# Gates stored sixteen keys to a row, and sixteen gathered rows moved to a later stage, in a decoder block on one core

## The chip, the cores and the metric

The kernel runs on one core of a Trainium2 chip. The metric is the device time of one execution in microseconds (us); lower is better. The engines are PE (TensorE, matmul; its weight loads are shown as PEld), DVE (VectorE), ACT (ScalarE), POOL (GpSimd) and SP (SyncE, which here only issues DMAs). Each engine works through its own instructions in order; 16 DMA engines move the data.

## The reference

One decoder block on x of shape (1, 512, 1024): an RWKV-7 group beside sliding-window attention, then PEER, a mixer that retrieves experts by product keys. The change lies in PEER alone, on 4 blocks of 128 tokens:

```python
def block(x_b):
    q = (x_b @ wq).reshape(-1, H, 2, PEER_HALF).astype(f32)
    s = jnp.einsum('thcd,hcnd->thcn', q, subkeys.astype(f32))
    s_top, i_top = lax.top_k(s, K)
    cand_s = (s_top[:, :, 0, :, None] + s_top[:, :, 1, None, :]).reshape(-1, H, K * K)
    cand_i = (i_top[:, :, 0, :, None] * PEER_N_KEYS + i_top[:, :, 1, None, :]).reshape(-1, H, K * K)
    best_s, best_pos = lax.top_k(cand_s, K)
    idx = jnp.take_along_axis(cand_i, best_pos, axis=-1).reshape(-1, H * K)
    gate = jax.nn.softmax(best_s, axis=-1).reshape(-1, H * K).astype(x_b.dtype)
    u = u_tab[idx]
    act = jax.nn.gelu(jnp.einsum('td,ted->te', x_b, u), approximate=False)
    return jnp.einsum('te,ted->td', gate * act, v_tab[idx])
```

H is 8 heads, K 16 choices, so 128 experts of 16384 for each token. An expert's number is 128 times its first key plus its second key.

## The kernel before

PEER is computed in two ways at once. **Tokens 128 to 511** (three blocks, `ND` = 384 tokens) are computed densely: every one of the 16384 experts is multiplied with every token, and a gate, zero where the expert was not chosen, takes out the rest. The experts are handled in 128 blocks of 128. For block b the *u-product* (`up_product`, tile pA, lines L176 to L178 in the helper `mm3_`) multiplies the 128 vectors u with the 384 tokens: 24 matmuls, since every factor is split into a high and a low part (`split`, L166 on ACT for the high part uh, L167 on DVE for the low part ul). A Gelu (L969) makes act of it. In the main part, act times gate is `w_` (`weigh`, L1312 on POOL), which is split into wh and wl, and is multiplied with the vectors v of the block, split into vh and vl (`accumulate`, L1357 to L1359, tile acc, 18 matmuls a block).

**Tokens 0 to 127** are computed by gathering: for each of the 128 choices j, `gather(j)` lets POOL issue an indirect DMA that fetches one row of 1024 numbers for each token (L1169, 512 KB in all, four buffers), first from u (j from 0 to 127), then from v (128 to 255). `gathered(j)` multiplies it on DVE: a u row with h2g (L1182, tile scr, sum into ac), a v row with ac, added to x (L1180).

The order on each engine is the order in which the code is written (a manual schedule). The stages from 580 us on are:

- **The gates' stage** (`for n in range(8 * NTC)`, 96 units). Unit n makes the gates of four tokens: DVE writes one-hot tiles O (L1228) and P (L1233), three units ahead; PE multiplies them in eight matmuls (L1255, tile pG); ACT copies the result into the tile gst (L1256). After eight units a chunk of 32 tokens, 2 MB, is written to DRAM by SP (L1266). Between the units run 69 steps of u-products made ahead (a step is 12 matmuls, so two make one block; SP loads its u at L796), whose act is kept in SBUF or spilled to DRAM (actd, acts). And `EARLY` gathered rows are asked for, spread evenly over the 96 units; each is multiplied three requests later.
- **The turn**: the last chunk is written in eight pieces (one at L1266, seven at L1336), ten more steps of u-products run, and the first gates (`gate_load`, L1296, tile gts, 12 loads for four blocks) and v (L1304) are loaded.
- **The main part** (`for b in range(127)`): each iteration loads three blocks ahead (`load`), splits block b + 1 (`prepare_block`), weighs block b + 2, accumulates block b, and computes the u-product of block 22 + b where it was not made ahead: 64 of the iterations, the others are single ones. Then come the rows asked for one iteration earlier, and new requests up to `upto(b)`, which shares 256 - `EARLY` rows out over blocks 0 to 120, twice as many to an iteration with a u-product as to a single one. After the last rows the norm of tokens 0 to 127 follows, and at the end that of the others (`residual`).

The gates in DRAM are an array (n, 128, GW x TC) for each chunk: second key in the middle, and GW first keys with TC = 32 tokens each side by side in a row; `NG` = 128 / GW. GI = 4 first keys are read at once, 512 bytes a partition.

Of the kernel before, what the change touches and what calls it, by code (L numbers as in the profile page):

```python
# [64 lines left out]
SPILL = [RING + (i * (128 - RING)) // NSPILL for i in range(NSPILL)]  # L65
AHEAD_UP = list(range(RING)) + SPILL

EARLY = 44


def peer_block_kernel(tc, A, out, dbg=None, stop=None):
    with ExitStack() as ctx:
        _emit(ctx, tc, A, out, dbg or {}, stop)


def _emit(ctx, tc, A, out, dbg, stop):
# [1026 lines left out]
    def steps(gen, n):  # L1103
        for _ in range(n):
            next(gen, None)
# [60 lines left out]
    def gather(j):  # L1166
        r_ = gp_.tile([128, D], F32, name="row", tag="row", bufs=4)
        w_, jj = j // 128, j % 128
        GP.indirect_dma_start(r_, None, A["vB"].rearrange("b p d -> (b p) d") if w_ else A["u"],  # L1169
                              bass.IndirectOffsetOnAxis(ap=ix[:, w_, jj:jj + 1], axis=0))  # L1170
        rows[j] = r_

    def gathered(j):
# [7 lines left out]
        else:  # L1181
            V.scalar_tensor_tensor(scr, r_, 1.0, h2g, op0=OP.mult, op1=OP.mult, accum_out=ac[:, jj:jj + 1])  # L1182


    TC, GI, GW = 32, 4, 8
    NG = 128 // GW
    NTC = ND // TC

    NG0 = 2
    gd = [[nc.dram_tensor(f"gates{t}_{g0}", (n, 128, GW * TC), F32, kind="Internal").ap() for g0, n in  # L1190
           (((0, NG0), (NG0, NG - NG0)) if t == NTC - 1 else ((0, NG),))] for t in range(NTC)]
    hot = {}
# [46 lines left out]
    for n in range(3):  # L1239
        one_hots(n)  # L1240
    def pieces(ci):
        return ([(0, NG0)] + [(g, 2) for g in range(NG0, NG, 2)]) if ci == NTC - 1 else [(0, NG)]

    done = asked = 0
    left = 2 * len(AHEAD_UP) - sum(UPS1) - sum(UPST) - BEHIND
    for n in range(8 * NTC):
        one_hots(n + 3)
        O, P = hot.pop(n)
        ci, t4 = n // 8, n % 8
        if t4 == 0:  # L1250
            gst = tk.tile([128, NG, GW, TC], F32, name="gst", tag="gst", bufs=2)
        p = psT.tile([128, 4, 128], F32, name="pG", tag=("sel", "pq", "psc")[n % 3], bufs=2)
        for u in range(4):
            for i in range(2):
                mm(p[:, u, :], O[:, u // 2, 0, :, u % 2], P[:, u // 2, i, :, u % 2], start=i == 0, stop=i == 1)  # L1255
        SC.activation(gst[:, :, :, t4 * 4:t4 * 4 + 4].rearrange("p n g t -> p (n g) t"),  # L1256
                      p.rearrange("p t e -> p e t"), AF.Copy, scale=1.0 / GS)
        if t4 == 7:

            writes = []  # L1260
            for g0, n_ in pieces(ci):
                d = gd[ci][g0 >= NG0 and ci == NTC - 1]
                d0 = NG0 if d.shape[0] == NG - NG0 else 0
                writes.append((d[g0 - d0:g0 - d0 + n_].rearrange("n p x -> p n x"),
                               gst[:, g0:g0 + n_].rearrange("p n g t -> p n (g t)")))
            SY.dma_start(*writes.pop(0))  # L1266
        steps(ups, (n + 1) * left // (8 * NTC) - n * left // (8 * NTC))
        while asked < (n + 1) * EARLY // (8 * NTC):
            gather(asked)
            asked += 1  # L1270
            if asked > 3:
                gathered(done)
                done += 1
# [11 lines left out]
    def upto(b):  # L1285

        return min(256, EARLY + (256 - EARLY) * sum(cost[:b + 1]) // sum(cost[:LASTG + 1]))

    vs, ws, gts = {}, {}, {}

    def gate_load(g):
        gts[g] = pv_.tile([128, NTC, GI, TC], F32, name="gts", tag="gts", bufs=2)
        for i in range(NTC):
            n, part = g // (GW // GI), g % (GW // GI)
            d, n = (gd[i][0], n) if len(gd[i]) == 1 or n < NG0 else (gd[i][1], n - NG0)
            SY.dma_start(gts[g][:, i], d[n, :, part * GI * TC:(part + 1) * GI * TC].rearrange("p (g t) -> p g t", t=TC))  # L1296
# [191 lines left out]
```

## Time and profile before

| what | value |
|---|---|
| time, median of 3 runs | 1629.78 us (1628.6 to 1633.54) |
| the profiled execution | 1630.73 us |
| its span, first to last instruction | 1629.0 us |
| granted TensorE clock, mean of the span | 0.995 |
| PE busy | 1572.6 us, 97% |
| DVE busy | 1286.1 us, 79% |
| POOL busy | 742.4 us, 46% |
| ACT busy | 652.5 us, 40% |
| moved by DMA | 371.18 MB, 228 GB/s over the span |

The busy times are sums over the whole span; what bounds a stage is read from the stage. Windows give them for a stretch, a timeline the single instructions, and the waits say for what an engine stood still.

### The profile page before, as it was taken

To read this page: it belongs to the slowest core of one execution; us is meant where nothing else is said; L and a number is where in the kernel's file an instruction comes from. 1 tells how busy PE (TensorE), PEld (TensorE's weight loads), DVE (VectorE), ACT (ScalarE), POOL (GpSimd) and SP (SyncE) were. 2 spreads that over 40 slices of the span, in tenths; PEclk is the share of its full clock that TensorE was granted. 3 is DMA by queue.
4 is the path that set the end of the run, shared out by engine and by line. 5 is a ranking of instruction groups with operands and counts; after the bars stand their busy time and mean duration, and the time that the engine had idled before them with its cause. 6 is when DMAs were issued, how large, how long until landed. Compare 5 with 4: busy or idle time off the path is not lost.

```text
span 1629.0 us, 30768 instructions
## 1 busy us (share of the span) xinstructions
PE 1572.6 (97%) x11869; PEld 1366.7 (84%) x11869; DVE 1286.1 (79%) x2497; ACT 652.5 (40%) x1092; POOL 742.4 (46%) x711
## 2 busy tenths in 40 slices
PE   7999999899999889999999999999999999999997
PEld 4777777797999888888988888888888888888886
DVE  6666567756899999999677788777878877887896
ACT  5333345544444344454433333333333333333334
POOL 5121123244676512222155555555655556556582
PEclk9999999999999999999999999999999999999999
DMA  4111110333232269999999888889998988989793
GB/s 143 53 42 42 59 48 2 129 124 103 79 104 91 98 214 336 348 323 354 320 345 351 304 309 320 322 299 316 331 308 301 333 312 303 321 303 339 236 311 136
DMA packets 180548, 371.18 MB, mean 228 GB/s; under 512 B 17840, under 2 KB 102320, under 8 KB 180144
## 3 DMA queue, kind: packets, MB, share of 16 engines
q1 hardware_dynamic: 137488, 226.71, 40.6%
q0 software_dynamic: 36864, 134.23, 22.9%
q10 hardware_dynamic: 6048, 8.26, 1.4%
q8 instruction: 93, 1.52, 0.4%
q14 instruction: 55, 0.45, 0.1%
HBM read 333.62 MB, written 35.52 MB: 227 GB/s over the span
## 4 chain that ended last, share of the span: by engine, by line
PE 50%; DVE 11%; DMA 3%; issue 1%; ACT 1%; POOL 1%; SPq 0%; DVEq 0%; ACTq 0%
PE acc L1359 10%; PE acc L1358 10%; PE acc L1357 10%; PE pA L178 7%; PE pA L176 7%; PE pA L177 7%; DVE O L1228 3%; DVE ul L167 2%; DVE scr L1182 2%; DVE P L1233 2%; DMA u<-in_uT_dram 2%; DMA row<-in_vB_dram,ix 1%; DMA v<-in_vB_dram 0%; PE pG L1255 0%; POOL row L1169 0%
## 5 line engine op out<-in xcount | busy, mean ns | idle before, releaser
L178 PE MATMUL pA<-h2hi,ul 128*128 128x384 f32 x1024 | 346.2, 338 | 9.9 <-DVE ul L167 5.6
L176 PE MATMUL pA<-h2hi,uh 128*128 128x384 f32 x1024 | 350.3, 342 | 1.5 <-ACT actd L969 1.5
L177 PE MATMUL pA<-h2lo,uh 128*128 128x384 f32 x1024 | 344.1, 336 | 0.0
L1169 POOL DMA_INDIRECT row<-in_u_dram,ix x128 | 175.2, 1369 | 285.7 <-DVE scr L1182 247.7
L1359 PE MATMUL acc<-vl,wh 128*128 128x512 f32 x768 | 300.3, 391 | 1.5 <-DVE vl L167 1.5
L1358 PE MATMUL acc<-vh,wl 128*128 128x512 f32 x768 | 300.0, 391 | 0.2 <-DVE wl L167 0.2
L1357 PE MATMUL acc<-vh,wh 128*128 128x512 f32 x768 | 298.9, 389 | 1.3 <-ACT vh L166 1.3
L1169 POOL DMA_INDIRECT row<-in_vB_dram,ix x128 | 196.1, 1532 | 141.1 <-DVE x L1180 115.7
L167 DVE TENSOR_TENSOR vl<-v,vh 128x1024 fp32r<-128x1024 f32 x128 | 213.9, 1672 | 35.2 <-ACT vh L166 34.4
L178 PEld LDWEIGHTS pA<-h2hi,ul 128*128 128x128 f32 x1024 | 192.8, 188 | 14.8 <-DVE ul L167 10.5
L176 PEld LDWEIGHTS pA<-h2hi,uh 128*128 128x128 f32 x1024 | 193.0, 188 | 4.7 <-ACT actd L969 1.6
L177 PEld LDWEIGHTS pA<-h2lo,uh 128*128 128x128 f32 x1024 | 193.2, 189 | 3.0
L1180 DVE SCALAR_TENSOR_TENSOR x<-row,ac,x 128x1024 f32<-128x1024 f32 x128 | 173.2, 1353 | 7.9 <-DMA row<-in_vB_dram,ix 6.0
L1359 PEld LDWEIGHTS acc<-vl,wh 128*128 128x128 f32 x768 | 144.1, 188 | 32.2 <-DVE vl L167 2.2
L1357 PEld LDWEIGHTS acc<-vh,wh 128*128 128x128 f32 x768 | 144.2, 188 | 30.0 <-ACT vh L166 1.6
L1358 PEld LDWEIGHTS acc<-vh,wl 128*128 128x128 f32 x768 | 144.1, 188 | 29.4 <-DVE wl L167 0.6
L1182 DVE SCALAR_TENSOR_TENSOR scr<-row,h2g 128x1024 f32<-128x1024 f32 x128 | 158.2, 1236 | 1.3
L166 ACT CAST uh<-u 128x1024 fp32r<-128x1024 f32 x128 | 133.9, 1046 | 62.2 <-PE pA L177 29.5
L167 DVE TENSOR_TENSOR ul<-u,uh 128x1024 fp32r<-128x1024 f32 x109 | 134.0, 1230 | 20.1 <-ACT uh L166 17.0
L166 ACT CAST vh<-v 128x1024 fp32r<-128x1024 f32 x128 | 134.0, 1048 | 0.3 <-DMA gts<-gates 0.3
L969 ACT ACTIVATE act<-pA 128x384 f32<-128x384 f32 x86 | 42.2, 491 | 131.6 <-PE pA L178 131.5
L1256 ACT ACTIVATE gst<-pG 128x512 f32<-128x512 f32 x96 | 55.8, 597 | 97.6 <-PE pG L1255 95.9
(725 smaller groups left out, 2621.0 us busy)
## 6 DMA issues: line engine op xcount, KB each, us to landing
u<-in_uT_dram SPq DMA_DIRECT2D x128, 512.0 KB, 6.4
v<-in_vB_dram SPq DMA_DIRECT2D x128, 512.0 KB, 5.9
gts<-gates SPq DMA_DIRECT2D x384, 64.0 KB, 4.5
gates<-gst SPq DMA_DIRECT2D x11, 2048.0 KB, 11.5
w<-in_w_in_dram SPq DMA_DIRECT2D x40, 256.0 KB, 2.8
wq<-in_wq_dram SPq DMA_DIRECT2D x16, 512.0 KB
acts<-actd ACTq DMA_DIRECT2D x42, 192.0 KB, 6.3
act<-acts SPq DMA_DIRECT2D x42, 192.0 KB, 7.5
```

The costliest lines, as they stand in the source:

```text
L166: (hi_eng or SC.copy)(dst_hi, src)
L167: (lo_eng or V).tensor_tensor(out=dst_lo, in0=src, in1=dst_hi.bitcast(F32), op=OP.subtract)
L176: mm(ps, whi[k][:, :m], ahi[:, k], start=k == 0, stop=False)
L177: mm(ps, whi[k][:, :m], alo[:, k], start=False, stop=False)
L178: mm(ps, wlo[k][:, :m], ahi[:, k], start=False, stop=k == KD - 1)
L1169: GP.indirect_dma_start(r_, None, A["vB"].rearrange("b p d -> (b p) d") if w_ else A["u"], bass.IndirectOffsetOnAxis(ap=ix[:, w_, jj:jj + ...
L1180: V.scalar_tensor_tensor(x2[:, 0, :], r_, ac[:, jj:jj + 1], x2[:, 0, :], op0=OP.mult, op1=OP.add)
L1182: V.scalar_tensor_tensor(scr, r_, 1.0, h2g, op0=OP.mult, op1=OP.mult, accum_out=ac[:, jj:jj + 1])
L1256: SC.activation(gst[:, :, :, t4 * 4:t4 * 4 + 4].rearrange("p n g t -> p (n g) t"), p.rearrange("p t e -> p e t"), AF.Copy, scale=1.0 / GS)
L1357: mm(o, wh[:, ts], vh[:, ds_], start=b == 0, stop=False)
L1358: mm(o, wl[:, ts], vh[:, ds_], start=False, stop=False)
L1359: mm(o, wh[:, ts], vl[:, ds_], start=False, stop=b == 127)
```

## The change

In a row of the stored gates stand 16 first keys instead of 8 (`GW`), so a row is 2 KB instead of 1 KB and a chunk has 8 times 128 rows instead of 16 times 128. The tile in SBUF has the same bytes in the same places. The last chunk's pieces are one row group each instead of two, of the same 256 KB. `EARLY` falls from 44 to 28: 28 rows are asked for in the gates' stage, 228 instead of 212 in the main part.

```diff
-EARLY = 44
+EARLY = 28
...
-    TC, GI, GW = 32, 4, 8
+    TC, GI, GW = 32, 4, 16
     NG = 128 // GW
     NTC = ND // TC
 
-    NG0 = 2
+    NG0 = 1
     gd = [[nc.dram_tensor(f"gates{t}_{g0}", (n, 128, GW * TC), F32, kind="Internal").ap() for g0, n in
            (((0, NG0), (NG0, NG - NG0)) if t == NTC - 1 else ((0, NG),))] for t in range(NTC)]
...
     def pieces(ci):
-        return ([(0, NG0)] + [(g, 2) for g in range(NG0, NG, 2)]) if ci == NTC - 1 else [(0, NG)]
+        return ([(0, NG0)] + [(g, 1) for g in range(NG0, NG)]) if ci == NTC - 1 else [(0, NG)]
```

DVE in the gates' stage, before, about the ninth unit: O and P are the one-hot tiles, ul a split, scr a gathered row (tiles with their numbers).

```order
L1228 TENSOR_TENSOR O_7669<-iota2_4455,sK_7449 128x1024
L1233 TENSOR_TENSOR P_7670<-O_7669,sG_7450 128x1024
L1228 TENSOR_TENSOR O_7684<-iota2_4455,sK_7449 128x1024
L1233 TENSOR_TENSOR P_7685<-O_7684,sG_7450 128x1024
L1182 SCALAR_TENSOR_TENSOR scr_7447,ac_7446<-row_7551,h2g_4451 128x1024
L1228 TENSOR_TENSOR O_7714<-iota2_4455,sK_7449 128x1024
L1233 TENSOR_TENSOR P_7715<-O_7714,sG_7450 128x1024
L167 TENSOR_TENSOR ul_7731<-u_7581,uh_7730 128x1024
L1228 TENSOR_TENSOR O_7750<-iota2_4455,sK_7449 128x1024
L1233 TENSOR_TENSOR P_7751<-O_7750,sG_7450 128x1024
L1182 SCALAR_TENSOR_TENSOR scr_7447,ac_7446<-row_7603,h2g_4451 128x1024
```

The same place on DVE with the change:

```order
L1228 TENSOR_TENSOR O_7667<-iota2_4455,sK_7449 128x1024
L1233 TENSOR_TENSOR P_7668<-O_7667,sG_7450 128x1024
L1228 TENSOR_TENSOR O_7682<-iota2_4455,sK_7449 128x1024
L1233 TENSOR_TENSOR P_7683<-O_7682,sG_7450 128x1024
L1228 TENSOR_TENSOR O_7709<-iota2_4455,sK_7449 128x1024
L1233 TENSOR_TENSOR P_7710<-O_7709,sG_7450 128x1024
L167 TENSOR_TENSOR ul_7726<-u_7581,uh_7725 128x1024
L1228 TENSOR_TENSOR O_7745<-iota2_4455,sK_7449 128x1024
L1233 TENSOR_TENSOR P_7746<-O_7745,sG_7450 128x1024
L1228 TENSOR_TENSOR O_7761<-iota2_4455,sK_7449 128x1024
L1233 TENSOR_TENSOR P_7762<-O_7761,sG_7450 128x1024
```

The two rows are gone from here: the first row now follows the 14th unit instead of the ninth, and later ones are further apart. O, P and ul keep their order.

SP at the end of the gates' stage, as a difference (a minus is before, a plus is the change; the square brackets name what the DMA waits for): the last chunk's writes among the loads of u.

```order
-L1266 DMA gates_0<-gst 128x2x256 [waits DMAHW5_49,Activation_49]
+L1266 DMA gates_0<-gst 128x512 [waits DMAHW5_49,Activation_49]
 L796 DMA u<-in_uT_dram 128x1024 [waits DMAHW6_49,DMAHW4_49,DVE_49]
-L1336 DMA gates_2<-gst 128x2x256 [waits DMAHW0_49]
-L1336 DMA gates_2<-gst 128x2x256 [waits DMAHW1_49]
+L1336 DMA gates_1<-gst 128x512 [waits DMAHW0_49]
+L1336 DMA gates_1<-gst 128x512 [waits DMAHW1_49]
 L796 DMA u<-in_uT_dram 128x1024 [waits DMAHW2_49,DVE_49]
```

Only the shape of the writes differs; their number, place and waits are the same.

DVE in the last blocks of the main part, before (x is a gathered v row, wl and vl are the splits of the next block; "x2" stands for two in a row):

```order
L1180 SCALAR_TENSOR_TENSOR x_4450<-row,ac,x_4450 128x1024 x2
L167 TENSOR_TENSOR wl<-w__17081,wh 128x384
L167 TENSOR_TENSOR vl<-v,vh 128x1024
L1180 SCALAR_TENSOR_TENSOR x_4450<-row,ac,x_4450 128x1024
L167 TENSOR_TENSOR wl<-w__17115,wh 128x384
L167 TENSOR_TENSOR vl<-v,vh 128x1024
L1180 SCALAR_TENSOR_TENSOR x_4450<-row,ac,x_4450 128x1024
L167 TENSOR_TENSOR wl<-w__17161,wh 128x384
L167 TENSOR_TENSOR vl<-v,vh 128x1024
```

The same blocks with the change:

```order
L1180 SCALAR_TENSOR_TENSOR x_4450<-row,ac,x_4450 128x1024
L167 TENSOR_TENSOR wl<-w__17079,wh 128x384
L167 TENSOR_TENSOR vl<-v,vh 128x1024
L1180 SCALAR_TENSOR_TENSOR x_4450<-row,ac,x_4450 128x1024
L167 TENSOR_TENSOR wl<-w__17112,wh 128x384
L167 TENSOR_TENSOR vl<-v,vh 128x1024
L1180 SCALAR_TENSOR_TENSOR x_4450<-row,ac,x_4450 128x1024 x2
L167 TENSOR_TENSOR wl<-w__17160,wh 128x384
L167 TENSOR_TENSOR vl<-v,vh 128x1024
```

Blocks with two rows stand at other places and a little more often; over the whole main part, 32 of the 64 iterations with a u-product ask for three rows instead of 20, and 11 of the other 57 that have rows ask for two instead of 7.

## Rows read from the trace of the kernel before

**Rows 1.** The page: busy tenths of an engine, and of the DMA engines, in 40 equal slices of the span (40.7 us each).

```profile
PE   7999999899999889999999999999999999999997
DVE  6666567756899999999677788777878877887896
DMA  4111110333232269999999888889998988989793
```

**Rows 2.** Windows of 40 us in the gates' stage: length, then busy us (and number of instructions) of PE, PEld, DVE, ACT and POOL, the granted clock, the share of the DMA engines that is busy, and GB/s.

```profile
600.00:640.00 40.00, 38.90 (x318) 36.21 (x318) 39.38 (x59) 20.33 (x33) 9.18 (x8) 1.00 0.98 340
640.00:680.00 40.00, 37.08 (x297) 33.71 (x296) 38.91 (x59) 18.82 (x34) 9.38 (x8) 1.00 0.94 334
680.00:720.00 40.00, 36.97 (x293) 32.74 (x291) 39.41 (x59) 18.33 (x32) 9.19 (x8) 1.00 0.99 357
720.00:760.00 40.00, 37.66 (x303) 34.51 (x302) 39.31 (x59) 20.76 (x35) 9.18 (x8) 1.00 0.89 317
```

**Rows 3.** Timeline of PE: start in us, duration, engine, line, operation and tiles, how many in one; the matmuls of the gates' units (eight a unit), from the third unit to the tenth, and the last unit.

```profile
586.63 0.64 PE L1255 MATMUL pG<-P,O 128*128 128x128 f16 x8
...
589.28 1.09 PE L1255 MATMUL pG<-P,O 128*128 128x128 f16 x16
...
592.35 0.64 PE L1255 MATMUL pG<-P,O 128*128 128x128 f16 x8
...
595.00 0.64 PE L1255 MATMUL pG<-P,O 128*128 128x128 f16 x8
...
597.61 1.10 PE L1255 MATMUL pG<-P,O 128*128 128x128 f16 x16
...
600.69 0.64 PE L1255 MATMUL pG<-P,O 128*128 128x128 f16 x8
...
793.18 0.64 PE L1255 MATMUL pG<-P,O 128*128 128x128 f16 x8
```

**Rows 4.** Timeline of DVE in the gates' stage, one after the other.

```profile
702.45 0.69 DVE L1228 TENSOR_TENSOR O<-iota,sK 128x1024 f16<-128x1024 f16 x1
...
703.17 0.69 DVE L1233 TENSOR_TENSOR P<-O,sG 128x1024 f16<-128x1024 f16 x1
...
703.77 0.69 DVE L1228 TENSOR_TENSOR O<-iota,sK 128x1024 f16<-128x1024 f16 x1
...
704.50 0.69 DVE L1233 TENSOR_TENSOR P<-O,sG 128x1024 f16<-128x1024 f16 x1
...
705.11 1.22 DVE L167 TENSOR_TENSOR ul<-u,uh 128x1024 fp32r<-128x1024 f32 x1
...
706.24 1.22 DVE L1182 SCALAR_TENSOR_TENSOR scr<-row,h2g 128x1024 f32<-128x1024 f32 x1
...
707.38 0.08 DVE L1182 DVE_READ_ACCUMULATOR scr<-row,h2g 128x1 f32 x1
```

**Rows 5.** Groups by line and shape from 580 to 800 us: busy us and mean ns of one, then the idle time of the engine just before them and what ended it.

```profile
L1169 POOL DMA_INDIRECT row<-in_u_dram,ix x44 | 51.1, 1162 | 185.8 <-DVE scr L1182 162.2 <-DVE ix L1155 20.0 <-DVE rest L1213 2.7
L1182 DVE SCALAR_TENSOR_TENSOR scr<-row,h2g 128x1024 f32<-128x1024 f32 x41 | 49.9, 1218 | 0.0
```

**Rows 6.** DMA from 580 to 800 us: queues with packets, MB and the share of 16 engines (q0 is POOL's queue, with the gathers; q10 is ACT's, with the stores of actd, 1.5 KB a partition; q1 is SP's), and one group of issues with their number and size.

```profile
q1 hardware_dynamic: 27785, 40.87, 54.2%
q0 software_dynamic: 6336, 23.07, 27.9%
q10 hardware_dynamic: 4979, 6.81, 8.6%
...
u<-in_uT_dram SPq DMA_DIRECT2D x34, 512.0 KB, 12.8
```

**Rows 7.** Timeline of PE at the start of the main part; in square brackets the idle time before and what ended it.

```profile
820.15 0.50 PE L1357 MATMUL acc<-vh,wh 128*128 128x512 f32 x1 [1.32 <-ACT vh L166]
...
821.70 0.50 PE L1359 MATMUL acc<-vl,wh 128*128 128x512 f32 x1 [0.83 <-DVE vl L167]
```

**Rows 8.** Windows from the turn to the last blocks, columns as in rows 2.

```profile
795.00:820.00 25.00, 23.83 (x138) 23.51 (x136) 8.90 (x9) 8.41 (x13) 3.79 (x4) 1.00 0.93 310
...
840.00:900.00 60.00, 60.00 (x293) 53.09 (x293) 45.38 (x58) 20.40 (x28) 35.40 (x27) 1.00 0.97 351
900.00:1200.00 300.00, 300.00 (x1473) 267.33 (x1472) 236.08 (x270) 107.62 (x148) 170.16 (x129) 1.00 0.90 313
1200.00:1500.00 300.00, 300.00 (x1472) 267.28 (x1471) 241.12 (x202) 105.14 (x145) 174.53 (x129) 1.00 0.91 316
...
1560.00:1600.00 40.00, 39.22 (x173) 31.93 (x172) 33.45 (x31) 15.20 (x24) 29.51 (x19) 1.00 0.86 295
```

**Rows 9.** Waits from 800 us to the end: who waited for whom, us in total, times, the longest.

```profile
ACT wh L166 <- PE acc L1359: 349.8, 119, 3.7
...
DVE x L1180 <- DMA row<-in_vB_dram,ix: 6.0, 5, 2.5
```

**Rows 10.** A gathered v row in the main part: the durations of its multiplication in ns (least, median, most) with the first and last start; and the group of its gathers on POOL.

```profile
L1180 DVE SCALAR_TENSOR_TENSOR x<-row,ac,x x128: 1269/1284/2050, 1138.8 to 1596.7; 128x1024 f32<-128x1024 f32 x128
...
L1169 POOL DMA_INDIRECT row<-in_vB_dram,ix x128 | 196.1, 1532 | 141.1 <-DVE x L1180 115.7 <-issue 7.2 <-DVE scr L1182 5.9
```

**Rows 11.** Timeline of DVE in the last blocks: two gathered rows, the second with the time that DVE waited for it.

```profile
1560.08 2.04 DVE L1180 SCALAR_TENSOR_TENSOR x<-row,ac,x 128x1024 f32<-128x1024 f32 x1
...
1596.72 1.28 DVE L1180 SCALAR_TENSOR_TENSOR x<-row,ac,x 128x1024 f32<-128x1024 f32 x1 [2.52 <-DMA row<-in_vB_dram,ix]
```

## The prediction

> **What bounds the kernel now.** I read the page first: engine totals and the slices of the span. PE is busy nearly everywhere, but DVE reaches 9 tenths in only one stretch, slices 13 to 18, where DMA is at 9 too [rows 1]. That is the gates' stage, so I read it by windows. In 600 to 760 us DVE is busy 39.38 + 38.91 + 39.41 + 39.31 = 157.0 of 160 us, PE a little less, and the DMA engines 0.89 to 0.99 of the time [rows 2]. A busy PE says little, since matmul ends are modelled; its pace says more. The stage is 96 units; each multiplies eight matmuls pG, and 69 steps of the u-products (12 matmuls) are spread between them. From the ninth unit on, gathered rows are multiplied in between. Before that, from 586.63 to 600.69, seven units passed (56 matmuls pG): 14.06 / 7 = 2.009 us each. From 600.69, the tenth unit, to 793.18, the 96th, there are 86 units: 192.49 / 86 = 2.238 us each [rows 3]. PE's own work is the same in both stretches. So the stage with rows is 0.229 us a unit above PE's pace, 19.7 us in all, and the engine that is full there is DVE.
>
> DVE's own steps are read from start to start: two units take O, P, O, P in 2.66 us (702.45 to 705.11), the split ul 1.13, a gathered row 1.14 [rows 4]. 41 of the 44 rows asked for are multiplied in the stage [rows 5].
>
> After 820 us the picture turns. PE is busy 60.00 of 60 and 300.00 of 300 us with DVE at 0.76 to 0.80 and DMA at 0.90 to 0.97 [rows 8]. The waits say who is ahead of whom: ACT, before it splits the next block's weights, waited 349.8 us, 119 times and up to 3.7 us, for PE to free the buffer; DVE waited 6.0 us in all for a gathered row [rows 9]. The data of the main part lie ready before PE wants them.
>
> **The change, step by step.** (1) *Sixteen rows fewer in the stage.* 25 instead of 41 are multiplied, the first in the 14th unit instead of the ninth. DVE loses 16 x 1.14 = 18.2 us, so the 86 units need 192.5 - 18.2 = 174.3 us of it. In units 9 to 12, which had rows and now have none, DVE needs about 1.33 + 0.36 x 1.13 = 1.74 us a unit (one ul to two steps, 69 steps on 96 units) against PE's 2.01, and loses 4 x 0.27 = 1.1 us waiting: 175.4. PE needs 86 x 2.009 = 172.8. Now the two are nearly equal. DVE was idle 3.0 us in 160 before [rows 2]; if it idles as often again, 3.3 us, the stretch takes 178.7. So the gain lies between 192.5 - 178.7 = 13.8 and 17.1, with 19.7 as the end that PE sets. I take **15.5**: some of the idle time stays, because in-order engines with equal work still meet at ul and P.
>
> POOL issues 16 gathers fewer there, 1.16 us each [rows 5], and is idle most of the time: nothing.
>
> (2) *DMA in the stage.* 44 gathers took 27.9% of 16 engines over 220 us, that is 982 us of engine time, 22.3 for each, or 1.40 us of all sixteen; with 128 packets of 4 KB in a gather that is 0.174 us a packet. The queue of the actd stores moves 1.5 KB packets: 302.7 us for about 4430, 0.068 each. On the third queue 34 u-loads and one more load, 4480 packets of 4 KB at 0.174, leave 1908 - 780 = 1128 us and 22.5 MB, about 22000 packets of 1 KB, for the gates: 0.051 [rows 6]. A 2 KB packet then costs, scaled from 1.5 KB or drawn between 1 and 4 KB, 0.091 to 0.092, against 0.102 for two of 1 KB; a 2 MB chunk needs 1024 x 0.091 / 16 = 5.8 us instead of 6.5. Per unit DMA was needed 0.95 x 2.238 = 2.13 us; it loses 16 x 1.40 / 86 = 0.26 and 0.7 / 8 = 0.09: 1.78, below PE's 2.01. So DMA stays beside the work, and I give the wider packets nothing here.
>
> The Trainium skill ("DMA: Bandwidth & Descriptors", section on why small descriptors are slow) names a fixed overhead of about 3 cycles a packet beside 32 bytes a cycle; by that, 2 KB in one packet is 67 cycles against 70, a saving of 4%, not the 10% of the rows. By it the next term would be nearer to nothing; the sum would be 1616.2 instead of 1615.2.
>
> (3) *The turn to the main part.* After the last unit PE has ten steps of u-products as cover while the last chunk is written in eight pieces and the first gates and v come back. The cover is about 2 us too short: PE waits 1.32 us for vh and 0.83 for vl [rows 7], the end of a chain of transfers at a DMA share of 0.93 [rows 8]. One chunk is 0.7 us cheaper and fewer rows are in flight. Between 0 and 2.15 gained, I take **1.0**.
>
> (4) *Sixteen rows more in the main part.* Blocks 0 to 120 ask for 228 rows instead of 212. Each costs DVE 1.28 us (median, 2.05 at most) and POOL 1.53 [rows 10], and 1.40 us of all DMA engines: 16 x 1.40 = 22.4 us over some 780, so 0.905 becomes about 0.93. DVE: 16 x 1.28 = 20.5, from 0.79 to 0.82. What hides it is the lead of up to 3.7 us per block [rows 9] and a stretch, 840 to 900, that already moved 351 GB/s at a share of 0.97 with PE full [rows 8]. The thin place is the last blocks, single ones of about 4.1 us: there a row takes DVE 2.04 us at times, and one came 2.52 us late [rows 11]. Blocks 106 to 120 ask for 19 rows instead of 18. Between 0 and 6.6 us (two rows at 2.04 and one more late by 2.5); nearer to 0, since PE lost only 0.78 of the 40 us there [rows 8]: **1.0**.
>
> The gathers keep their order, all other instructions too; the gates' loads still read 512-byte pieces, only 2 KB apart instead of 1 KB, and I cost that at nothing: the lead of the blocks covers it, and without that cover it is part of rival C.
>
> *Sum:* 15.5 + 1.0 - 1.0 = 15.5 us. The profiled execution took 1630.73 (span 1629.0), 0.95 above the median of the runs, 1629.78: 1615.2 on its own clock, **1614.5** against the median.
>
> **The rivals.**
> A. *The main part pays on DVE and POOL.* A late or slow row stands ahead of the splits wl and vl in DVE's queue, and PE waits for vl. If each of the 16 rows costs the difference between the slowest and the median, 2.05 - 1.28 = 0.77, PE loses 12.3 us and the gain shrinks to 16.5 - 12.3 = 4.2: 1625.6. For it: the late row and PE's wait at the end [rows 11, 8]. Against it: median 1284 beside a maximum of 2050 [rows 10], and none of PE's idle time between 840 and 1560. The Trainium skill ("SBUF — State Buffer", section "two separate sides", on the port pair that DVE and GpSimd share) says that a DVE instruction with two inputs from SBUF and a GpSimd instruction that reads it lock each other out for a whole instruction; the spread of L1180 agrees, and by that rule this loss grows with POOL's work.
>
> B. *The u-loads hold the stage.* PE's pace of 2.009 was read before the first chunk was written, where DMA was little used. If the 2 MB writes, ahead of the u-loads in SP's queue, hold u back by 1 us a chunk, 11 us of the gain stay away: 1625.5. For it: DMA at 0.98 in 600 to 640 [rows 2]. Against it: DVE, not DMA, was full, and DMA's need falls by a sixth.
>
> C. *Slower: DMA becomes the bound of the main part.* 16 rows are 8.4 MB, 26.7 us at 314 GB/s. If PE had to wait for all of it, 26.7 - 16.5 = 10.2 us slower: 1640. For it: a share of 0.90 over 600 us. Against it: 351 GB/s in 840 to 900 with PE full [rows 8], where 314 x 1.033 = 324 is wanted. It decides once over 16.5 of the 26.7 us reach PE.
>
> D. *No effect.* Whoever lets PE wait in the stage is not DVE, and the pace stays 2.24: 1629. Against it: rows 2 and 4.
>
> **How the numbers follow.** Forecast 0.75, rival A 0.07, B 0.08, C 0.07, D 0.03. A measurement of this kernel can tell about 0.3%, 4.9 us, from no change. Faster by more: the forecast, half of B and a part of A (where the loss stays smaller): 0.75 + 0.04 + 0.02 = 0.81; within 0.3%: the rest of A and B, and D, 0.05 + 0.04 + 0.03 = 0.12; slower: C, 0.07. The range: downward PE's pace in the whole stage, no wait in the turn and none in the main part, 19.7 + 2.15 = 21.9, hardly all at once: 1609; upward to the near parts of A and B: 1624.
>
> **What would show it.** Right: some 2.04 to 2.08 us a unit from the tenth to the last; DVE below 0.97 there, DMA at or below 0.9; the main part PE full with ACT still waiting for PE over 300 us. Wrong: a pace of 2.15 or more, with PE waiting for ul behind a late u (B); PE waiting for vl or wl in many blocks after 840 (A); idle PE behind v or gts, DMA at 0.97 and more over hundreds of us (C).

## The result, and the profile after

The changed kernel took 1621.07 us (median of 6 runs, 1617.46 to 1621.87) against 1631.57 us before (6 runs, 1628.6 to 1635.42): a ratio of 0.9932, with a 95% interval of 0.9916 to 0.9948. It is 10.5 us faster, inside the range forecast (1609 to 1624) and 5 us short of the 15.5 us of the sum. The profiled execution took 1620.6 us, its span 1618.9 us, so it stands for the median.

The page, busy tenths in 40 slices (compare [rows 1]):

```profile
PE   7999999999999889999999999999999999999997
DVE  6766557756899989999578887888888788888877
DMA  4111110342232358999999999898999989989783
```

The gates' stage is still the one where DVE and DMA both stand at 9. The windows there, columns as in [rows 2]:

```profile
600.00:640.00 40.00, 40.00 (x336) 37.79 (x334) 37.09 (x53) 20.62 (x34) 4.67 (x4) 1.00 0.86 297
640.00:680.00 40.00, 39.10 (x317) 36.24 (x314) 38.87 (x58) 21.29 (x39) 6.87 (x6) 1.00 0.91 328
680.00:720.00 40.00, 39.71 (x324) 37.02 (x323) 39.23 (x59) 20.98 (x38) 5.73 (x5) 1.00 0.90 317
720.00:760.00 40.00, 39.65 (x327) 36.73 (x326) 39.34 (x58) 20.37 (x34) 6.88 (x6) 1.00 0.96 343
```

PE now gets 317 to 336 matmuls done in 40 us, before 293 to 318. DVE is no longer alone at the top: PE is full in the first window, where four rows are multiplied (eight before), and DVE is at 38.87 to 39.34 in the other three, with five or six rows each. The pace says it exactly. The tenth and the last unit on PE (compare [rows 3]):

```profile
599.81 0.65 PE L1255 MATMUL pG<-P,O 128*128 128x128 f16 x8
...
778.39 0.64 PE L1255 MATMUL pG<-P,O 128*128 128x128 f16 x8
```

(778.39 - 599.81) / 86 = 2.077 us a unit, against 2.238 before.

The start of the main part on PE, with the idle time in square brackets (compare [rows 7]), and a window of what follows:

```profile
803.71 0.34 PE L178 MATMUL pA<-h2hi,ul 128*128 128x384 f32 x1
805.13 0.50 PE L1357 MATMUL acc<-vh,wh 128*128 128x512 f32 x1 [1.08 <-ACT vh L166]
805.46 0.39 PE L1358 MATMUL acc<-vh,wl 128*128 128x512 f32 x1
806.68 0.50 PE L1359 MATMUL acc<-vl,wh 128*128 128x512 f32 x1 [0.83 <-DVE vl L167]
...
808.74 0.63 PE L1359 MATMUL acc<-vl,wh 128*128 128x512 f32 x1
809.16 0.63 PE L1357 MATMUL acc<-vh,wh 128*128 128x512 f32 x1
...
812.51 0.40 PE L1359 MATMUL acc<-vl,wh 128*128 128x512 f32 x1
```

```profile
808.00:812.00 4.00, 4.00 (x13) 3.14 (x12) 2.64 (x3) 2.76 (x4) 0.00 (x0) 0.64 1.03 396
```

The wait for vh is 1.08 instead of 1.32 us, the one for vl the same 0.83. But after the two pauses the matmuls follow each other in 0.42 us (808.74 to 809.16) instead of 0.23, and the granted clock is 0.64 over these 4 us, between its levels of 1.2 and 2.4 GHz. Before, the same pauses were followed by a clock of 1.00.

Windows of the main part (compare [rows 8]) and the two waits of [rows 9], here from 785 us:

```profile
840.00:900.00 60.00, 60.00 (x295) 53.30 (x294) 49.35 (x58) 22.16 (x31) 36.83 (x28) 1.00 0.95 337
900.00:1200.00 300.00, 300.00 (x1474) 267.47 (x1473) 250.44 (x286) 104.71 (x145) 178.10 (x135) 1.00 0.92 328
1200.00:1500.00 300.00, 300.00 (x1470) 266.97 (x1469) 252.79 (x207) 106.01 (x146) 179.01 (x136) 1.00 0.92 324
1560.00:1600.00 40.00, 37.62 (x163) 30.08 (x162) 31.91 (x31) 16.01 (x24) 22.64 (x15) 1.00 0.66 230
```

```profile
ACT wh L166 <- PE acc L1359: 360.8, 122, 4.5
...
DVE x L1180 <- DMA row<-in_vB_dram,ix: 11.4, 10, 2.7
```

From 840 to 1500 us PE is as full as before, with DVE at 0.82 to 0.84 and DMA at 0.92 to 0.95. In the last blocks it lost 2.38 of 40 us, where it had lost 0.78, and DVE's wait for late rows has nearly doubled.

Following the same events on PE in both traces cuts the difference into stretches (us; the blocks are counted by their first matmul acc):

| stretch | before | after | difference |
|---|---|---|---|
| start to the first unit | 581.72 | 579.81 | -1.9 |
| first unit to the tenth | 18.97 | 20.00 | +1.0 |
| tenth unit to the last | 192.49 | 178.58 | -13.9 |
| last unit to the first acc (the turn) | 26.97 | 26.74 | -0.2 |
| block 0 to block 10 | 71.61 | 73.21 | +1.6 |
| block 10 to block 105 | 628.52 | 628.52 | 0.0 |
| block 105 to the last acc | 99.25 | 102.55 | +3.3 |
| last acc to the end | 9.50 | 9.49 | 0.0 |

Together -10.1, as the spans. The first two stretches hold nothing of the change but the first chunk's write: all the work ahead of the first unit is the same, and up to the tenth the profile shows a granted clock of 0.86 instead of 0.91 in 580 to 600 us, a value that lay anywhere from 0.83 to 0.91 in the runs below.

The +3.3 us at the end can be seen instruction by instruction. First DVE, then POOL, then PE in the same stretch of the changed kernel:

```profile
1546.66 1.28 DVE L1180 SCALAR_TENSOR_TENSOR x<-row,ac,x 128x1024 f32<-128x1024 f32 x1
1550.45 1.29 DVE L1180 SCALAR_TENSOR_TENSOR x<-row,ac,x 128x1024 f32<-128x1024 f32 x1 [2.51 <-DMA row<-in_vB_dram,ix]
1551.65 0.55 DVE L167 TENSOR_TENSOR wl<-w__17012,wh 128x384 fp32r<-128x384 f32 x1
1552.12 1.22 DVE L167 TENSOR_TENSOR vl<-v,vh 128x1024 fp32r<-128x1024 f32 x1
```

```profile
1539.68 1.79 POOL L1169 DMA_INDIRECT row<-in_vB_dram,ix  x1
1541.78 1.69 POOL L1169 DMA_INDIRECT row<-in_vB_dram,ix  x1 [0.31 <-issue]
```

```profile
1551.92 0.39 PE L1357 MATMUL acc<-vh,wh 128*128 128x512 f32 x1
1552.26 0.51 PE L1358 MATMUL acc<-vh,wl 128*128 128x512 f32 x1
1553.39 0.50 PE L1359 MATMUL acc<-vl,wh 128*128 128x512 f32 x1 [0.63 <-DVE vl L167]
```

POOL issued two gathers one behind the other. DVE multiplied the first row at 1546.66 and then stood 2.51 us until the second was there, 8.7 us after POOL had begun it. Behind that row in DVE's queue stand wl and vl of the next block, and PE waited for them. The second gather began 2.1 us after the first and took 8.6 us from issue to landing, where the median of all v rows is 6.7. The same happens two more times, with waits of 2.67 and 1.16 us for the row: blocks 115, 119 and 123 take 5.24, 5.95 and 5.69 us instead of 4.08, 4.08 and 5.43. By the code, the single blocks at the end ask for a pair of rows in blocks 108, 112, 116 and 120; before, they did so in 107, 114 and 120. Each stall comes three blocks after a pair, but the first pair of the change and the first two of before were followed by none.

### The profile page after: what moved, and what is told of

Its sections match the earlier page's. It is cut to its first block, busy times and chain, and to the rows that moved or that the text cites. A ratio compares the mean times of both kernels' runs of the same rounds, so it can differ in the third digit from the quotient of the medians.

```text
span 1618.9 us, 30804 instructions
## 1 busy us (share of the span) xinstructions
PE 1572.4 (97%) x11869; PEld 1370.0 (85%) x11869; DVE 1300.6 (80%) x2497; ACT 651.3 (40%) x1092; POOL 738.1 (46%) x711
## 4 chain that ended last, share of the span: by engine, by line
PE 52%; DVE 9%; DMA 3%; issue 1%; POOL 1%; ACT 1%; SPq 0%; DVEq 0%; ACTq 0%
PE acc L1359 10%; PE acc L1358 10%; PE acc L1357 10%; PE pA L178 7%; PE pA L176 7%; PE pA L177 7%; DVE O L1228 2%; DVE ul L167 2%; DVE P L1233 2%; DMA row<-in_vB_dram,ix 1%; DVE scr L1182 1%; DMA u<-in_uT_dram 1%; PE pG L1255 1%; POOL row L1169 1%; ACT uh L166 0%
## 5 line engine op out<-in xcount | busy, mean ns | idle before, releaser
L1169 POOL DMA_INDIRECT row<-in_vB_dram,ix x128 | 185.8, 1451 | 146.8 <-DVE x L1180 114.0
L167 DVE TENSOR_TENSOR vl<-v,vh 128x1024 fp32r<-128x1024 f32 x128 | 219.2, 1713 | 31.9 <-ACT vh L166 29.8
L167 DVE TENSOR_TENSOR ul<-u,uh 128x1024 fp32r<-128x1024 f32 x109 | 139.8, 1284 | 22.7 <-ACT uh L166 22.3
```

What stands on the lines that cost most here:

```text
L167: (lo_eng or V).tensor_tensor(out=dst_lo, in0=src, in1=dst_hi.bitcast(F32), op=OP.subtract)
```

## The experiments

**The change once more**, run beside the experiments: how far its profile repeats.

> The changed kernel once more, as the measure for its neighbours on the same chip. About 10 us faster than before (ratio 0.9935, 0.992 to 0.995). Open is the slow first block of the main part, which took 6.93 us instead of 5.35 while the granted clock fell to 0.64 in 808 to 812 us. If that belongs to the change, block 0 takes about 6.9 us here too; if it is chance, 5.3 to 5.4 with the clock at 1.00. The stalls of PE in blocks 115 and 119 (1.2 and 1.9 us) should be there again in either case, since they come from the order on DVE.

1621.08 us against 1631.92 before, ratio 0.9930 [0.9912, 0.9947]. The profiled execution was the slowest of the six, 1627.31 us. In it the pace in the stage was 2.079 us a unit, and blocks 115, 119 and 123 took 5.51, 5.85 and 6.01 us. What does not repeat is the start of the main part: here the first pause on PE was 2.97 us (from the start of one matmul to the start of the next; 1.42 in the profile above), and block 0 took 8.1 us after it.

**The wider rows alone**, and **the 28 rows alone**, as differences from the change:

```diff
-EARLY = 28
+EARLY = 44
```

> Only the storage: sixteen keys to a row, 44 rows in the gates' stage as before. Theory (DVE is the bound of that stage, DMA lies beside it): pace 2.22 to 2.24 us a unit from the tenth unit on, time within 2 us of before (0.9985 to 1.001), DMA share in the stage lower by some 0.03 to 0.06. Rival (DMA was the bound): pace 2.15 or less and at least 6 us faster.

```diff
-    TC, GI, GW = 32, 4, 16
+    TC, GI, GW = 32, 4, 8
...
-    NG0 = 1
+    NG0 = 2
```

> Only the rows: 28 in the gates' stage, gates stored eight keys to a row as before. Theory (DVE): pace 2.07 to 2.09 us a unit as with the whole change, about 10 us faster than before (0.992 to 0.995). Rival (the packets carry a good part): pace 2.12 or more, at most 6 us faster.

The storage alone: 1633.27 us, ratio 1.0001 [0.9991, 1.0011], pace 2.239. The rows alone: 1622.02 us, ratio 0.9935 [0.9920, 0.9950], pace 2.083. So the whole gain is that of the rows, and the storage neither gives nor takes a measurable part. A window of the first shows the stage of before, unchanged:

```profile
680.00:720.00 40.00, 36.96 (x289) 32.96 (x289) 39.41 (x59) 18.38 (x34) 9.17 (x8) 1.00 0.99 363
```

The wider packets did make the transfers cheaper. SP's queue from 605 to 775 us, with packets, MB and the share of 16 engines, first before, then with the wider rows alone (the same nine chunks in each):

```profile
q1 hardware_dynamic: 22952, 33.89, 58.2%
```

```profile
q1 hardware_dynamic: 13448, 33.64, 55.7%
```

That is 2.5 points, some 0.4 of them for the smaller number of bytes; 2.1% of 170 us over nine chunks is 0.40 us a chunk, and the pair with 28 rows (62.5% with 36.70 MB, 59.6% with 36.85 MB, ten chunks) gives 0.5. Against the 6.5 us that the prediction gave a chunk, this is 6 to 8%.

**Which resource held the stage?** Two kernels on the basis of before split a gathered row into its two halves. In the first, 16 rows are fetched in the stage and not multiplied; in the second, 16 rows are not fetched, and DVE multiplies a tile that is there instead. Each was timed in one execution only.

```diff
+    apart = [j for j in range(41) if (j + 1) * 16 // 41 > j * 16 // 41]
...
-        else:
+        elif j not in apart:
```

> The kernel before, 44 rows fetched in the gates' stage, but sixteen of them, spread evenly, are not multiplied there (left out of the computation; their sums stay zero). DVE is freed as by the change, DMA carries all it did. Theory (DVE is the bound): pace 2.06 to 2.09 us a unit from the tenth unit on. Rival (the DMA engines, at 0.95, are): 2.2 or more. For the clock in the turn: if the short pause of PE there is longer only with 2 KB rows, it is 1.3 to 1.7 us before the first matmul of the main part here and block 0 takes 5.3.

```diff
+        if j in apart:
+            rows[j] = x2[:, 1, :]
+            return
```

> The counterpart: 44 rows multiplied in the gates' stage as before, but sixteen of them are not fetched; DVE multiplies a tile of the same shape that lies in SBUF instead (so these sixteen sums are wrong). DMA is freed as by the change, DVE has all its work. Theory (DVE): pace 2.22 to 2.24, as before. Rival (DMA): 2.1 or less. The pause in the turn as in the run before this one.

Without the fetching nothing moved: 1631.72 us, pace 2.239. Two windows of it:

```profile
680.00:720.00 40.00, 36.94 (x288) 32.65 (x288) 39.38 (x59) 18.80 (x33) 5.73 (x5) 1.00 0.96 334
720.00:760.00 40.00, 37.74 (x304) 34.75 (x303) 39.34 (x59) 19.38 (x33) 4.59 (x4) 1.00 0.76 265
```

DMA had room (0.76), DVE was full (39.34 of 40), PE did as many matmuls as before. That settles the first bound: it is DVE, and DMA is not in front of it.

Without the multiplying, 1627.29 us, pace 2.153, between the expectation and its rival: only (2.238 - 2.153) x 86 = 7.3 of the change's 13.9 us. Two windows, the wait of ACT for u (600 to 780 us), and one of DVE's waits behind it:

```profile
640.00:680.00 40.00, 37.45 (x300) 33.75 (x298) 35.70 (x53) 18.58 (x34) 9.49 (x8) 1.00 0.93 336
680.00:720.00 40.00, 38.75 (x315) 36.16 (x313) 39.27 (x59) 21.22 (x38) 9.93 (x8) 1.00 0.97 352
```

```profile
ACT uh L166 <- DMA u<-in_uT_dram: 13.2, 5, 4.2
```

```profile
666.30 1.22 DVE L167 TENSOR_TENSOR ul<-u,uh 128x1024 fp32r<-128x1024 f32 x1 [3.24 <-ACT uh L166]
```

In the first window DVE has room (35.70) and PE still waits: ACT waits for u, 13.2 us in all and up to 4.2, where it waited 6.4 us before and 4.6 after. DVE, where ul stands ahead of O and P, waited 6.6 us for uh (1.4 with the change) and 2.1 for a gathered row. So a late u took most of what is missing here, what rival B describes. But this edit does more than leave out 16 multiplications. A row's buffer comes free when the row has been multiplied, and that had spread the gathers; without it POOL issues them in bursts. First POOL before, then in this run:

```profile
613.74 1.15 POOL L1169 DMA_INDIRECT row<-in_u_dram,ix  x1 [5.12 <-DVE scr L1182]
618.67 1.15 POOL L1169 DMA_INDIRECT row<-in_u_dram,ix  x1 [3.79 <-DVE scr L1182]
```

```profile
625.58 0.94 POOL L1171 DMA_INDIRECT row<-in_u_dram,ix  x1 [9.55 <-DMA row<-in_u_dram,ix]
626.82 0.94 POOL L1171 DMA_INDIRECT row<-in_u_dram,ix  x1 [0.30 <-issue]
628.06 0.93 POOL L1171 DMA_INDIRECT row<-in_u_dram,ix  x1 [0.30 <-issue]
```

Before, the gathers of the stage from 602 us on began 3.6 to 6.5 us apart; here two or three begin 1.2 to 2.4 us apart, and then none for 7 to 12 us. Whether u would also be late with the same rows fetched evenly is therefore not shown.

The same with rows of 2 KB asks whether the late u is a matter of the packets:

```diff
-EARLY = 28
+EARLY = 44
...
-        else:
+        elif j not in apart:
```

> 44 rows fetched, sixteen of them not multiplied in the gates' stage (left out of the computation), now with the gates in rows of 2 KB. With rows of 1 KB the pace was 2.153, half of the way, and ACT waited 13.2 us for u. Theory (once DVE is freed, the DMA engines are the next bound, and 2 KB packets relieve them by some 0.5 us a chunk): 2.09 to 2.15. Rival (packet size does not matter there at all, the late u came from the order of the transfers): 2.15 or more.

1628.52 us in its one execution, pace 2.148, at the border between the expectation and its rival. ACT's wait for u is nearly halved, 7.3 us in 600 to 780, and the pace is the same; the gathers come in the same bursts. So the wider packets do not bring the rest of the gain. Whether u is late since the DMA engines are full, since it stands behind a 2 MB chunk in SP's queue, or since the gathers are bunched, these runs don't tell apart.

**The last blocks with one row each.** If the pairs of gathers make the end slower, sharing the rows out evenly there must bring it back.

```diff
-    cost = [4 if RING + b in fresh else 2 for b in range(127)]
+    cost = [40 if RING + b in fresh else 20 if RING + b < 128 else 15 for b in range(127)]
```

> The change, with the sharing of rows in the main part altered so that each of the last fifteen single blocks asks for one row and none for two (weights 40, 20 and 15 instead of 4, 2 and 2); the four or so rows that this frees are asked for earlier, beside u-products. Theory (PE loses 3 us there because the second of two rows asked for together comes late and stands before wl and vl on DVE): blocks 115, 119 and 123 take 4.08 us instead of 5.24, 5.95 and 5.70, so 3 to 4.6 us faster than the change, 0.990 to 0.9925 of before. Rival (DVE or DMA simply has too much to do in the last blocks, whatever the order): the stalls move to other blocks and less than 1.5 us is won.

1619.08 us (1614.73 to 1620.08), ratio 0.9910 [0.9893, 0.9926]. In the trace blocks 105 and 127 begin 94.05 us apart, with the change 98.7 (99.2 in its second profile): 4.65 us or more. DVE there, in order of time:

```profile
1543.16 1.27 DVE L1180 SCALAR_TENSOR_TENSOR x<-row,ac,x 128x1024 f32<-128x1024 f32 x1
1544.59 0.56 DVE L167 TENSOR_TENSOR wl<-w__16940,wh 128x384 fp32r<-128x384 f32 x1 [0.15 <-ACT wh L166]
1545.54 1.79 DVE L167 TENSOR_TENSOR vl<-v,vh 128x1024 fp32r<-128x1024 f32 x1 [0.39 <-ACT vh L166]
1547.25 1.27 DVE L1180 SCALAR_TENSOR_TENSOR x<-row,ac,x 128x1024 f32<-128x1024 f32 x1
1548.66 0.56 DVE L167 TENSOR_TENSOR wl<-w__16973,wh 128x384 fp32r<-128x384 f32 x1
```

One row stands between two blocks' splits, none is waited for, and from 830 us to the end PE waits for nothing. Before, block 123 was already off pace (5.43 instead of 4.08 us), so of the 4.65 us 3.3 are new with the change, and 1.35 mend the kernel before. In the times it is 2.0 us between the medians and 3.3 by the ratios (0.0020 of 1632), with intervals that overlap: the trace shows the mechanism, the size in the time is less sure. The edit takes away the pairs and with them four of the 19 rows of blocks 106 to 120, and does not tell the one from the other.

**Fewer rows still in the stage**, with the even end: 20, then 12 rows.

```diff
-EARLY = 28
+EARLY = 20
...
+    cost = [40 if RING + b in fresh else 20 if RING + b < 128 else 15 for b in range(127)]
```

> The change with one row in each of the last single blocks (weights 40, 20, 15) and 20 rows instead of 28 in the gates' stage. DVE needs 8 x 1.14 = 9.1 us less, some 165 us for 86 units, PE 172.8. Theory (with 28 rows DVE and PE are nearly equal, below that PE is the bound): pace 2.01 to 2.04, 3.5 to 5.5 us less than with 28, not 9; the main part hides the eight rows; 0.987 to 0.9895 of before. Rival (DVE alone sets the pace, or the main part charges for the rows): pace falls on to 1.98 or lower, or blocks of the main part grow by 3 us or more.

```diff
-EARLY = 28
+EARLY = 12
...
+    cost = [40 if RING + b in fresh else 20 if RING + b < 128 else 14 for b in range(127)]
```

> 12 rows in the gates' stage, 244 in the main part, one in each of the last single blocks. Theory (with 20 rows PE already ran without a gap, pace 2.031; the main part still has room): pace 2.01 to 2.03, at most 1.7 us won in the stage; every block from the second to the last at PE's own 4.1 or 8.3 us; within 2 us of the kernel with 20 rows. Rival (the main part is full): blocks grow, 3 us or more slower than with 20 rows.

20 rows: 1611.38 us (1610.5 to 1614.92) against 1632.63 before, ratio 0.9875 [0.9859, 0.9891]; pace 2.031. 12 rows: 1611.56 us, ratio 0.9866 [0.9839, 0.9893]; pace 2.031. Two windows with 20 rows:

```profile
640.00:680.00 40.00, 40.00 (x333) 37.78 (x333) 37.93 (x56) 21.80 (x39) 4.78 (x4) 1.00 0.88 319
680.00:720.00 40.00, 40.00 (x328) 37.64 (x326) 39.09 (x57) 21.09 (x38) 4.58 (x4) 1.00 0.88 305
```

PE is full, DVE has 1 to 2 us left in 40. This is the pace that the prediction read before the first row, 2.009, to about 1%; taking eight more rows out adds nothing, since PE in the stage waits for DVE no longer. The main part takes 244 rows and keeps its pace.

**20 rows without the wider storage** (the difference is from the kernel with 20 rows) asks whether the storage matters once DMA and DVE both have room, and whether it has to do with the pause before the main part.

```diff
-    TC, GI, GW = 32, 4, 16
+    TC, GI, GW = 32, 4, 8
```

> 20 rows and the even end, but the gates stored eight keys to a row as before. Theory (the storage is worth nothing in time once the rows are fewer): within 1.5 us of the same kernel with 2 KB rows, pace 2.03 to 2.05. Rival (PE is at its pace only because the packets are wider): pace 2.06 or more and 3 us slower.

1611.16 us, ratio 0.9859 [0.9832, 0.9886], pace 2.031: the same as with 2 KB. In its profile, the slowest of four executions (1615.33 us), the pause ahead of the first acc was 2.58 us and block 0 took 6.9 us, with the wider rows 0.63 and 5.3; but the change has 1.42 and 2.97 in two profiles of one kernel, the storage alone, of 2 KB, had 2.86, and the two halves of a row, both with 1 KB, 4.70 (fetched alone) and 0.17 (multiplied alone). The pause differs between executions and does not follow the row size.

**Two more steps of u-products as cover in the turn**, with 20 rows:

```diff
-BEHIND = 10
+BEHIND = 12
```

> As the run before it, with 12 instead of 10 steps of u-products kept for the turn (4.15 us of PE's work moved from the gates' stage behind it). Theory (PE stands still at the start of the main part because gates and v come 1.4 to 3 us too late, and the granted clock then falls for some us): the pause before the first matmul is under 0.5 us, the clock stays at 1.00 and block 0 takes 4.1 to 5.3; 2 to 4 us faster than with 10 steps. Rival (the transfers start later by as much as the cover is longer): the pause stays, and time moves by less than 1 us.

1617.86 us, ratio 0.9913 [0.9899, 0.9927]: 6.5 us slower than with ten steps, and the theory fell. ACT, and then PE:

```profile
801.11 1.04 ACT L166 CAST uh<-u 128x1024 fp32r<-128x1024 f32 x1 [10.54 <-DMA u<-in_uT_dram]
```

```profile
802.60 0.69 PE L176 MATMUL pA<-h2hi,uh 128*128 128x384 f32 x1 [5.01 <-ACT actd L969]
```

The u of the added steps stands in SP's queue behind the first gates and v of the main part. ACT waited 10.54 us for it, PE 5.01, and after that the granted clock was 0.52 in 804 to 808 us. So the two steps were put ahead of those loads:

```diff
+    steps(ups, 2)
     for b in range(3):
         load(b)
-    steps(ups, BEHIND - 6)
+    steps(ups, BEHIND - 8)
```

> 20 rows, even end and 12 steps kept for the turn, as in the run that lost time there, but two of the steps stand ahead of the first loads of gates and v, so that no load of u stands behind them in SP's queue. Theory (that run waited 10.5 us for the u-load that had slid behind 12 gates' loads and v): the 5 us pause is gone, none over 0.7 us is left, the clock stays at 1.00 in the turn; 1 to 3 us faster than with 10 steps. Rival (a longer cover only delays the loads): a pause of 2 us or more remains.

1611.89 us, ratio 0.9862 [0.9833, 0.9890]: the 6 us are back, and nothing clear beyond, where 1 to 3 us had been expected. The profiled execution was the slowest of the four, 1616.63 us. In it the pause before the main part is gone, but ACT and PE wait inside block 0, for the u of the main part's first u-product:

```profile
807.30 1.04 ACT L166 CAST uh<-u 128x1024 fp32r<-128x1024 f32 x1 [4.66 <-DMA u<-in_uT_dram]
```

```profile
808.79 0.52 PE L176 MATMUL pA<-h2hi,uh 128*128 128x384 f32 x1 [2.81 <-ACT actd L969]
```

The order of the loads was the cause of the loss, so that half of the theory holds. The cover itself gains nothing measurable. In this execution what the queue owes at this place is only waited for by another instruction; that the faster ones show the same is not known.

## Why the prediction was right, and where it was off

**The bound.** Right, and now shown: taking the 16 multiplications off DVE makes the stage faster, taking the 16 fetches off DMA does not.

**Step (1), the stage: 13.9 us measured, 15.5 taken, 13.8 to 17.1 as bounds.** The chosen value supposed that only some of DVE's idle time stays. The windows show otherwise: two engines with nearly the same need, PE at 39.10 to 39.71 and DVE at 38.87 to 39.34 of 40 us, still lose time to each other. Over the whole stretch DVE's idle time rose, from 3.5 us of 192.5 to 5.7 of 178.6. That the lower bound, 178.7, met the measured 178.6 is luck. It was meant as DVE idling as often as before, but the 192.5 us from which it takes the rows off already hold that idle time, so it is counted twice: the bound stands for 170.8 us of work (189.0 busy less 18.2) and 7.9 idle. Measured are 172.8 busy and 5.7 idle. The work is more than the sum said, among other things because 24 rows are multiplied between the tenth unit and the last instead of 39, 15 fewer and not 16. The end that PE sets, 19.7, was nearly reached with 20 rows: (2.238 - 2.031) x 86 = 17.8. The pace of 2.077 is in the 2.04 to 2.08 that was named as proof. DVE "below 0.97 there" holds by a hair over the whole stretch (172.84 of 178.58 us, 0.968), and not in its last three windows, 0.97 to 0.98. So the forecast that DVE and PE would be nearly equal holds, but it took eight rows fewer yet before PE was free of DVE.

**Step (2), DMA in the stage: nothing, as costed.** The storage alone is at 1.0001. The share, though, fell to 0.86 to 0.96, in two of four windows above the 0.9 expected. On the size of a packet, the fixed overhead that the Trainium skill names ("DMA: Bandwidth & Descriptors", section on why small descriptors are slow) gives a saving of 4% as an estimate, the rows of before 10%, and the runs show 6 to 8% of a chunk, between them. That DMA "stays beside the work" needs an addition. In the run without the multiplying, with all bytes in place and the gathers in bursts, u came late and half of the gain stayed away. Rival B did not come about with this change, where ACT's wait for u fell from 6.4 to 4.6 us; that u could never be late does not follow.

**Step (3), the turn: 0.2 measured, 1.0 taken, 0 to 2.15 as bounds.** The wait for vh fell by 0.24 us only, and in the second profile it was longer. The term was mis-sized: the pause there differs from run to run by more than the change gives.

**Step (4), the main part: a loss of 4.9 measured, 1.0 taken, 0 to 6.6 as bounds.** This is the term with the largest miss. Over 95 blocks the added rows cost nothing, as argued: DVE, DMA and POOL had the lead that [rows 9] show. Of the 4.9, 3.3 lie in the last blocks, at the place and by the mechanism that the prediction named: a row late by 2.5 us ahead of wl and vl, rival A in small. It was sized too low. The prediction counted one row more in blocks 106 to 120 and not where the pairs fall: before, one of three pairs did harm, with the change three of four, four blocks apart, and their blocks take 1.16, 1.87 and 0.26 us longer than before. With one row a block the stalls are gone, in every profile of a kernel with that end; the profiles with 28 rows and pairs all have them. What sets the harmful pairs apart from the harmless ones is not shown. The other 1.6 lie in block 0, where PE ran for some us at the lower clock after its two pauses. The prediction had no term for that, and it is not shown to belong to the change: with 44 rows block 0 took from 4.6 to 8.1 us in the profiles, with 28 from 5.3 to 8.1.

The other profile of the change and the run with 28 rows alone give 1621 to 1622 us as well, so the 15.5 was not missed by chance: 13.9 + 0.2 - 3.3 = 10.8 without block 0, and 10.5 in the medians. All three terms were too hopeful, by 1.6, 0.8 and 2.3 us; no error made up for another.

**Smaller slips in the working** change nothing of this. DVE stands at 9 tenths in slices 12 to 19 and once more in 39, and DMA is at 9 beside it only in 16 to 19, not from 13 on. Of the 41 and 25 rows given to the stage, two and one are multiplied in the turn. And 15.5 us off the median is 1614.3, not 1614.5.

**The best version found** is 20 rows in the stage and one row for each of the last blocks: 21 us faster than before (1611.38 against 1632.63), some 10 us faster than the change. Between the two profiled executions it is 9.2: the pace gives (2.077 - 2.031) x 86 = 4.0 us and the even end 4.65; the turn and block 0 give 2.4, with a pause of 0.63 us and no fall of the clock; and 1.8 are lost ahead of the tenth unit, where nothing was changed. The width of the stored rows makes no measurable difference.

## What to carry to other kernels

When work moves from a full stage to one with room, price it by the thinnest place of the stage it goes to, not by the mean: the added rows cost nothing over 95 blocks, and pairs of rows in the last short blocks took back a quarter of what the stage had gained. Go on past the point where two engines come out equal by their sums, since equal engines still wait for each other, and stop where the other engine is full in every window. And to learn which half of a piece of work holds a stage, take the halves away one at a time: one alone gave nothing here, the other half. Then look at what else such an edit moves: leaving out the multiplications also bunched the gathers, and so what held the other half stays open.

## What the runs showed of the hardware

**A short pause can cost more than itself.** At the start of the main part PE pauses twice, and in several executions the granted clock fell just after. With a first pause (start to start) of 2.58 to 4.70 us block 0 took 6.9 to 8.1 us; with 1.38 and 0.63 us it took 5.3 with the clock at 1.00. But a pause of 1.42 us led to 0.64 (the profile after) and one of 1.65 us did not (the profile before), so its length alone does not decide, and what does stays open. The price, against those 5.3 us, is 1.6 to 2.8 us.

**A gathered row's way is uneven.** Between 1535 and 1580 us the gathers of v rows took from 5.1 to 9.6 us from issue to landing, around a median of 6.7 in the whole main part. A pair adds 2.1 us, since POOL issues its second one so much later; the two together made up the 2.5 us for which DVE stood in its queue.

**A row is multiplied slowly beside a weigh.** The 2.04 us of [rows 11] have a pattern that the timelines of DVE and POOL show. Before, all 13 v rows whose multiplication began while POOL ran a weigh (L1312) took 1.91 to 2.05 us, and the other 115 took 1.27 to 1.29, beside a gather on POOL too. With the change it is 12 of 12 at 1.60 to 2.05, three more at 2.13 to 2.61 during which a weigh began, and 113 at 1.27 to 1.29. In all the profiles of these kernels no v row took over 1.29 us without a weigh beside it. This is the slow row of rival A; the sixteen added rows brought two more of them in this profile, not sixteen.
